# Dealing out the gather steps of the v stage by the weight megabytes that TensorE still has ahead of it

## The chip, the cores and the metric

The kernel runs on one core of one Trainium2 chip. The metric is the device time of one execution in microseconds. Three runs of the kernel before took 2020.26, 2021.27 and 2027.03 us; their median, 2021.27 us, is the time to compare with.

## The reference

The program is a trunk of two layers over 256 tokens of width 1024. A layer has a mixer (convolution and pooling in layer 0, sparse attention beside a gated recurrence in layer 1), a cross attention over 256 memory rows, and the part that matters here, a layer of 16,384 experts of which each token chooses 128 (16 for each of 8 heads):

```python
def peer_ffn(h, wq, sub_keys, u, v):
    ...
        top, pos = lax.top_k(cand, PEER_TOPK)
        eid = jnp.take_along_axis(cand_id, pos, axis=-1).reshape(PEER_BLOCK, PEER_HEADS * PEER_TOPK)
        g = jax.nn.softmax(top, axis=-1).reshape(PEER_BLOCK, PEER_HEADS * PEER_TOPK).astype(xb.dtype)
        act = jax.nn.gelu(jnp.einsum('td,ted->te', xb, u[eid]))
        return jnp.einsum('te,ted->td', g * act, v[eid])
```

So a chosen expert e adds g · gelu(x·u[e]) · v[e] to the token. u and v are 64 MB each in a layer.

## The kernel before

The expert layer is the function `peer`, called once in each layer. It treats the 256 tokens in two ways.

176 tokens (`TD`) are done densely: all of u and all of v go through TensorE (PE). u and v are cut into 64 *pairs* (`NPAIR`) of two blocks of 128 experts. One pair is a `raw` tile of 128 partitions by 2048 fp32 values, 1 MB (2 to the power of 20 bytes), which `load` (line 774) fetches by SP's queue into one of five buffers in turn. `u_range` (line 819) computes the u half: it loads a pair of u, does its two blocks of matmuls at line 827 with a `yield` after each, and lets ScalarE (ACT) apply gelu at line 833. `v_pair` (line 1118) does the v half: VectorE (DVE) multiplies the activations by the gate weights into a `wt` tile (line 1130, three buffers), and PE adds the products into the four PSUM banks `O` (line 1134). The first 20 pairs (`NFIRST`) keep their weighted activations in `af` and need no `wt`. The gate weights of the others lie in HBM (`gd`) and come back four pairs at a time into `gr` (line 1116, two buffers), by SP's queue too, one group ahead.

The other 80 tokens (`NG`, in groups of 64 and 16) are done by *gather steps*. The generator `gathered` (line 793) has 160 of them in a layer. One step is an indirect DMA on GpSimd's queue (POOL, line 790) that fetches one expert row for each of 128 partitions (128 rows of 4 KB), and one DVE instruction that uses it: in the first 80 steps a dot product with the token (line 797, `dots`), in the last 80 a weighted sum into `acc` (line 809; the first step of a group at line 807). The row tiles share eight buffers, so a gather is issued when the DVE instruction of the step eight before it is done. When a group's sums are complete, PE adds them into the result by the `fold` matmuls at line 1175, and the result is added to `h` at line 1184.

The order: the u pairs 0 to 19 run beside the choosing of the experts; the rest of their 40 halves, 19, carry one gather step each; then `spread` builds the gate weights with the u pairs 20 to 39 beside it and a step after every second turn, which makes another 19. The code has thus taken 38 steps when the *v stage* begins. The v stage goes through the 64 v pairs in an order written out in `order` (first six of the af pairs, then the pairs 20 to 63 with one more af pair after every third) and runs the last 24 u pairs, 40 to 63, beside the first 24 v pairs from 20 on: 88 MB through PE in all. After each v pair it takes one gather step, after every fourth pair two: 80 in the stage. What is left is taken after the loop, 42 steps.

DVE's order inside these loops is the order of the program (`manual_schedule`); the other engines' queues are ordered by the framework's scheduler, and each queue runs in order. In the loop a DVE step of iteration n therefore stands behind `wt` of iteration n and ahead of `wt` of iteration n+1, and `wt` waits until PE has freed the buffer of three `wt` before it.

Of the kernel before, what the change touches and what calls it, by code (L numbers as in the profile page):

```python
# [28 lines left out]
NPAIR = 64  # L29
TG = 16  # L30
NFIRST = 20
NACT = 20

GROUPS = ((0, 64), (64, 16))
NG = sum(n for _, n in GROUPS)
TD = T - NG
NHEAD = 6
GQ = 4
Q1 = 2.2
Q2 = 1.7  # L40
# [28 lines left out]
def trunk(ctx: ExitStack, tc: tile.TileContext, a: dict, out: bass.AP, dbg=None):  # L69
# [37 lines left out]
    def bank():  # L107
        return ps.tile([P, 512], F32, name="b", tag="ps", bufs=2)
# [625 lines left out]
    def peer(l, sq, fill=None):  # L734
        with ExitStack() as es:
# [35 lines left out]
            turn = [0, 0]  # L771


            def load(src):

                n = turn[0] % 5
                turn[0] += 1
                if n < 3:
                    raw = st.tile([P, 2048], F32, name="raw", tag="raw", bufs=3)
                else:  # L780
                    raw = cp.tile([P, 2048], F32, name="raw", tag=f"xT{n - 3}", bufs=1)
                nc.sync.dma_start(raw, src)
                return raw

            def rows(src, g, i):

                q = ("whi", "wlo")[turn[1] % 2]
                turn[1] += 1
                t = st.tile([P, D], F32, name="row", tag=q, bufs=4)
                nc.gpsimd.indirect_dma_start(t, None, src, bass.IndirectOffsetOnAxis(ap=g["gi"][:, i:i + 1], axis=0))  # L790
                return t

            def gathered():
                for g in gs_:
                    for i in range(g["n"]):
                        t = rows(u_rows, g, i)
                        nc.vector.tensor_tensor_reduce(t, t, g["xg"], 1.0, 0.0, OP.mult, OP.add, g["dots"][:, i:i + 1])  # L797
                        if i == g["n"] - 1:
                            nc.scalar.activation(g["dots"], g["dots"], AF.Gelu_apprx_tanh)
                            nc.vector.tensor_mul(g["gw"], g["gw"], g["dots"])  # L800
                        yield
                for gn, g in enumerate(gs_):
                    acc = g["acc"] = pp.tile([P, D], F32, name=f"acc{gn}", tag=f"ga{gn}")
                    for i in range(g["n"]):
                        t = rows(v_rows, g, i)
                        if i == 0:
                            nc.vector.tensor_scalar(acc, t, g["gw"][:, 0:1], None, op0=OP.mult)
                        else:
                            nc.vector.scalar_tensor_tensor(acc, t, g["gw"][:, i:i + 1], acc, op0=OP.mult, op1=OP.add)  # L809
                        yield  # L810
# [8 lines left out]
            def u_range(i, j):  # L819

                for i in range(i, j):
                    raw = load(a["peer_u"][l, i])
                    b = bank()
                    for c in range(2):
                        for k in range(KB):
                            o = c * 1024 + k * P
                            nc.tensor.matmul(b[:, c * TD:(c + 1) * TD], raw[:, o:o + P], xd[:, k], start=k == 0, stop=k == KB - 1)  # L827
                        if c == 1:
                            if i < NFIRST:
                                dst = af[:, 2 * i:2 * i + 2].rearrange("p c t -> p (c t)")  # L830
                            else:
                                dst = act[i] = pools["ex"].tile([P, 2 * TD], F32, name="act", bufs=NACT)
                            nc.scalar.activation(dst, b[:, :2 * TD], AF.Gelu_apprx_tanh)  # L833
                            done.append(dst)
                        yield
# [197 lines left out]
            us = u_range(0, NFIRST)  # L1033
            interleave(choose(), us, Q1)
            bg = gathered()

            def steps():
# [64 lines left out]
            us = u_range(NFIRST, NFIRST + NACT)  # L1102
# [10 lines left out]
            def weights_of(g):  # L1113
                if g < (NPAIR - NFIRST) // GQ:
                    gr[g] = vp.tile([P, TD // TG, GQ * 2 * TG], F32, name="gr", bufs=2)
                    nc.sync.dma_start(gr[g], gd[:, :, g * GQ * 2 * TG:(g + 1) * GQ * 2 * TG].rearrange("g p f -> p g f"))

            def v_pair(i, first, last):
                if i < NFIRST:
                    raw = load(a["peer_v"][l, i])  # L1120
                    wt = af[:, 2 * i:2 * i + 2]
                else:
                    g, j = divmod(i - NFIRST, GQ)
                    if j == 0:
                        weights_of(g + 1)
                    gv = gr[g][:, :, j * 2 * TG:(j + 1) * 2 * TG].rearrange("p g (c t) -> p c g t", c=2)
                    raw = load(a["peer_v"][l, i])
                    at = act.pop(i)
                    wt = vp.tile([P, 2, TD], F32, name="wt", bufs=3)
                    nc.vector.tensor_mul(wt.rearrange("p c (g t) -> p c g t", t=TG),  # L1130
                                         at.rearrange("p (c g t) -> p c g t", c=2, t=TG), gv)
                parts = [(c, j) for c in range(2) for j in range(KB)]
                for c, j in sorted(parts, key=lambda z: z[1]) if last else parts:
                    nc.tensor.matmul(O[j // 2][:, (j % 2) * TD:(j % 2 + 1) * TD], raw[:, c * 1024 + j * P:c * 1024 + (j + 1) * P],  # L1134
                                     wt[:, c], start=first and c == 0 and j % 2 == 0, stop=last and c == 1,
                                     skip_group_check=True)
                if last:
                    ready_sqrt(wt[:, 0, 0:1])


            order, late = list(range(NHEAD)), list(range(NHEAD, NFIRST))
            for i in range(NFIRST, NPAIR):
# [2 lines left out]
                    order.append(late.pop(0))  # L1145
            order += late
            us = u_range(NFIRST + NACT, NPAIR)
            with tc.manual_schedule(engines={nc.vector.engine}):
                for n, i in enumerate(order):
                    v_pair(i, n == 0, n == NPAIR - 1)  # L1150
                    if n == 1:
                        weights_of(0)
                    for _ in range(2 if n % 4 == 3 else 1):
                        next(bg, None)
                    if i >= NFIRST:
                        next(us, None)
                        next(us, None)
            for _ in bg:
                pass

# [58 lines left out]
    with ExitStack() as es:  # L1219
# [7 lines left out]
        left = [(l, c) for l in range(2) for c in range(8)]  # L1227
# [27 lines left out]
        dump("h_xa0", h)  # L1255
        fill(6)
    sq = peer(0, sq)
    dump("h_pe0", h)
    sq = odd_mixer(sq)
    dump("h_mix1", h)  # L1260
    with phase("kv1") as kp:
# [4 lines left out]
        sq = xattn(1, k1, v1, sq)  # L1266
    dump("h_xa1", h)
    sq = peer(1, sq)


# [101 lines left out]
```

## Time and profile before

| what | value |
|---|---|
| median of three runs | 2021.27 us |
| profiled execution, its own time | 2011.56 us |
| its span, first to last instruction | 2009.3 us |
| mean granted clock of PE | 0.97 |
| busy: PE, DVE, ACT, POOL | 1885.8, 1090.7, 447.2, 409.5 us |
| moved by DMA | 572.76 MB, mean 285 GB/s |
| v stage of layer 0, layer 1 (first to last matmul of line 1134) | 537 to 957, 1534 to 1954 us of the span |

Times inside the profile are microseconds from the first instruction. One engine's row gives busy time; a PE that is busy is not PE at its peak, because matmuls overlap. In a timeline row the first number is the start, the second the length of the merged pieces, and the bracket tells how long the engine had been idle before them and what it had waited for. Windows give, for a stretch, each engine's busy time, PE's granted clock as a share of full speed, the mean busy share of the 16 DMA engines (packets can overlap, so it can pass 1) and the bytes moved per second.

### The profile page before, as it was taken

Reading aid. Unit: us, or ns where it says so; the run is one execution under the profiler, and the core shown is the slowest. Engines: PE = TensorE matmul, PEld = TensorE weight load, DVE = VectorE, ACT = ScalarE, POOL = GpSimd, SP = SyncE. Lnnn points to the kernel's source line nnn. Section 1 sums busy time; section 2 is a strip of 40 time slices with the busy share of each in tenths; the row PEclk is TensorE's granted clock in tenths of the full one; section 3 lists DMA queues with packets and bytes.
Section 4 is the critical chain, followed back from the end, with each engine's and each line's share of the span. In section 5 each row is a group of like instructions: output and inputs, shape, how many; then the busy total and the mean of one; then the engine's idle time right before and its main releaser. Section 6 shows DMA issues by size and latency. Waiting matters only on the chain.

```text
span 2009.3 us, 33483 instructions
## 1 busy us (share of the span) xinstructions
PE 1885.8 (94%) x13818; PEld 1856.6 (92%) x13818; DVE 1090.7 (54%) x2494; ACT 447.2 (22%) x807; POOL 409.5 (20%) x360
## 2 busy tenths in 40 slices
PE   8999999999899999999299999999989999999992
PEld 7999999999899999999199899999989999999981
DVE  5765588676512222345878766985765121213467
ACT  6455442122100000000074455421221000000000
POOL 0000001432211111234600100014322121212344
PEclk9999999999999999999599999999999999999996
DMA  6554756999998899899863254579999889988997
GB/s 242 182 186 137 243 176 220 372 383 342 352 335 306 319 309 335 313 379 345 342 218 116 106 214 141 176 267 364 372 336 364 318 311 318 326 313 329 381 343 272
DMA packets 138631, 572.76 MB, mean 285 GB/s; under 512 B 12400, under 2 KB 47984, under 8 KB 94960
## 3 DMA queue, kind: packets, MB, share of 16 engines
q1 hardware_dynamic: 81008, 370.06, 50.6%
q0 software_dynamic: 46080, 167.79, 22.7%
q10 hardware_dynamic: 11392, 32.77, 4.3%
q8 instruction: 109, 1.79, 0.3%
q14 instruction: 42, 0.34, 0.0%
HBM read 549.48 MB, written 21.10 MB: 284 GB/s over the span
## 4 chain that ended last, share of the span: by engine, by line
PE 52%; issue 27%; DVE 8%; POOL 6%; DMA 5%; ACT 1%; DVEq 0%; POOLq 0%; ACTq 0%
PE O L1134 14%; PE b L148 13%; PE b L827 11%; PE b L163 7%; POOL row L790 6%; DMA row<-in_peer_ur_dram,gi 2%; DVE acc L809 2%; DMA row<-in_peer_v_dram,gi 1%; DMA kd<-kvs 1%; DVE row L797 1%; DMA vd<-kvs 1%; PE fb L869 1%; PE fb L312 1%; PE fa L281 1%; PE fb L552 1%
## 5 line engine op out<-in xcount | busy, mean ns | idle before, releaser
L827 PE MATMUL b<-xd,raw 128*128 128x176 f32 x4096 | 634.7, 315 | 0.7 <-ACT af L833 0.7
L827 PEld LDWEIGHTS b<-xd,raw 128*128 128x128 f32 x4096 | 618.1, 191 | 1.2 <-ACT af L833 1.2
L1134 PE MATMUL O<-wt,raw 128*128 128x176 f32 x2816 | 430.2, 313 | 0.0
L1134 PEld LDWEIGHTS O<-wt,raw 128*128 128x128 f32 x2816 | 422.6, 190 | 0.0
L1130 DVE TENSOR_TENSOR wt<-act,gr 128x352 f32<-128x352 f32 x88 | 46.2, 525 | 589.9 <-PE O L1134 563.7
L790 POOL DMA_INDIRECT row<-in_peer_ur_dram,gi x160 | 196.8, 1230 | 802.2 <-DVE dots L797 482.1
L790 POOL DMA_INDIRECT row<-in_peer_v_dram,gi x160 | 192.7, 1205 | 352.6 <-DVE acc L809 224.6
L148 PE MATMUL b<-xT,whi 128*128 128x256 f32 x1376 | 250.2, 283 | 2.8 <-DVE xT L129 2.4
L126 DVE TENSOR_TENSOR wlo<-raw,whi 128x1024 fp32r<-128x1024 f32 x158 | 191.2, 1220 | 101.6 <-ACT whi L125 100.9
L148 PEld LDWEIGHTS b<-xT,whi 128*128 128x128 f32 x1376 | 211.7, 189 | 5.2 <-DVE xT L129 3.8
L125 ACT ACTIVATE whi<-raw 128x1024 fp32r<-128x1024 f32 x158 | 166.1, 1060 | 217.7 <-PE b L148 117.9
L797 DVE CUSTOM_DVE_ANT_0 row<-row,xg 128x1024 f32<-128x1024 f32 x160 | 191.9, 1214 | 41.1 <-DMA row<-in_peer_ur_dram,gi 41.1
L809 DVE SCALAR_TENSOR_TENSOR acc<-row,gw,acc 128x1024 f32<-128x1024 f32 x156 | 200.1, 1283 | 7.7 <-DMA row<-in_peer_v_dram,gi 4.1
L1134 PE MATMUL O<-af,raw 128*128 128x176 f32 x1280 | 195.8, 313 | 0.0
L148 PE MATMUL b<-xT,wlo 128*128 128x256 f32 x688 | 192.5, 280 | 0.3 <-DVE wlo L126 0.3
L1134 PEld LDWEIGHTS O<-af,raw 128*128 128x128 f32 x1280 | 192.2, 190 | 0.0
L833 ACT ACTIVATE act<-b 128x352 f32<-128x352 f32 x88 | 40.9, 464 | 652.7 <-PE b L827 652.7
L148 PEld LDWEIGHTS b<-xT,wlo 128*128 128x128 f32 x688 | 129.7, 189 | 0.8 <-DVE wlo L126 0.5
L163 PE MATMUL b<-whi,y 128*128 128x256 f32 x512 | 89.4, 279 | 0.0
L1175 PE MATMUL b<-acc,fold 128*128 128x512 f32 x16 | 14.2, 1016 | 75.4 <-DVE acc L809 75.4
L1175 PEld LDWEIGHTS b<-acc,fold 128*128 128x128 f32 x16 | 4.2, 308 | 81.1 <-issue 44.3
L163 PEld LDWEIGHTS b<-whi,y 128*128 128x128 f32 x512 | 77.4, 188 | 0.4
(333 smaller groups left out, 1766.5 us busy)
## 6 DMA issues: line engine op xcount, KB each, us to landing
raw<-in_peer_u_dram SPq DMA_DIRECT2D x128, 1024.0 KB, 7.9
raw<-in_peer_v_dram SPq DMA_DIRECT2D x128, 1024.0 KB, 7.5
raw<-in_xattn_wkv_dram SPq DMA_DIRECT2D x16, 1024.0 KB, 5.0
raw<-in_peer_wq_dram SPq DMA_DIRECT2D x16, 1024.0 KB, 5.0
gd<-gs ACTq DMA_DIRECT2D x22, 704.0 KB, 8.7
gr<-gd SPq DMA_DIRECT2D x22, 704.0 KB, 9.7
raw<-in_odd_w_in_dram SPq DMA_DIRECT2D x15, 1024.0 KB, 4.9
raw<-in_even_w_in_dram SPq DMA_DIRECT2D x8, 1024.0 KB, 4.8
```

The costliest lines, as they stand in the source:

```text
L125: nc.scalar.activation(hi, src, AF.Copy)
L126: nc.vector.tensor_sub(lo, src, hi.bitcast(F32))
L148: nc.tensor.matmul(dst, w[j][p][:, k * P:(k + 1) * P], x[q][:, k, :], start=n == 0, stop=n == 3 * KB - 1)
L163: nc.tensor.matmul(dst, x[q][:, k, tb * P:(tb + 1) * P], wk[p][:, o:o + 256], start=n == 0, stop=n == 3 * KB - 1)
L281: nc.tensor.matmul(lg[:, tb * T:(tb + 1) * T], qT[p][:, 2 * hd + j, tb * P:(tb + 1) * P], kT[q][:, 2 * hd + j], start=n == 0, stop=n == 5)
L790: nc.gpsimd.indirect_dma_start(t, None, src, bass.IndirectOffsetOnAxis(ap=g["gi"][:, i:i + 1], axis=0))
L797: nc.vector.tensor_tensor_reduce(t, t, g["xg"], 1.0, 0.0, OP.mult, OP.add, g["dots"][:, i:i + 1])
L809: nc.vector.scalar_tensor_tensor(acc, t, g["gw"][:, i:i + 1], acc, op0=OP.mult, op1=OP.add)
L827: nc.tensor.matmul(b[:, c * TD:(c + 1) * TD], raw[:, o:o + P], xd[:, k], start=k == 0, stop=k == KB - 1)
L833: nc.scalar.activation(dst, b[:, :2 * TD], AF.Gelu_apprx_tanh)
L1130: nc.vector.tensor_mul(wt.rearrange("p c (g t) -> p c g t", t=TG), at.rearrange("p (c g t) -> p c g t", c=2, t=TG), gv)
L1134: nc.tensor.matmul(O[j // 2][:, (j % 2) * TD:(j % 2 + 1) * TD], raw[:, c * 1024 + j * P:c * 1024 + (j + 1) * P], wt[:, c], start=first and ...
```

## The change

It replaces the fixed deal of one step per iteration (two on every fourth) by a count in units of 1 MB of weights. A v pair is one unit, a u pair that runs beside it another, so the stage has 88 units. `left` is 85 of them, all but the last three (`NTAIL`), and `todo` is the number of gather steps not yet taken when the stage begins (`turn[1]` counts those that are), 160 − 38 = 122. Each unit adds `per` = 122/85 = 1.435 to `due`, and as many steps are taken as `due` holds whole ones. The u pair of an iteration now comes ahead of its gather steps in the program; before, it came behind them.

```diff
+NTAIL = 3
...
+            left, todo = 2 * NPAIR - NFIRST - NACT - NTAIL, 2 * NG - turn[1]
+            due, per = 0.0, todo / left
             with tc.manual_schedule(engines={nc.vector.engine}):
                 for n, i in enumerate(order):
                     v_pair(i, n == 0, n == NPAIR - 1)
                     if n == 1:
                         weights_of(0)
-                    for _ in range(2 if n % 4 == 3 else 1):
+                    due += per
+                    if i >= NFIRST and next(us, "no") != "no":
+                        next(us, None)
+                        due += per
+                    while due >= 1:
+                        due -= 1
                         next(bg, None)
-                    if i >= NFIRST:
-                        next(us, None)
-                        next(us, None)
             for _ in bg:
                 pass
```

Nothing else is changed; the steps, the loads and the matmuls are the same in number and kind.

## Rows read from the trace of the kernel before

**Rows 1.** The page: the span in 40 slices of 50 us, the busy share in tenths (9 is 90% or more) of PE and of the DMA engines.

```profile
PE   8999999999899999999299999999989999999992
...
DMA  6554756999998899899863254579999889988997
```

**Rows 2.** The timeline, in order of time, at the end of the expert layer of layer 0: start us, length us, engine, line, operation, written tile and read tiles, count, and in brackets the idle time before and its releaser.

```profile
938.64 17.13 DVE L809 SCALAR_TENSOR_TENSOR acc<-row,gw,acc 128x1024 f32<-128x1024 f32 x13
...
947.47 9.71 PE L1134 MATMUL O<-wt,raw 128*128 128x176 f32 x64
...
952.44 5.10 SPq L134 DMA_DIRECT2D raw<-in_odd_w_in_dram  x2
...
958.63 0.52 DVE L1164 COPY ob<-O 128x352 f32<-128x352 f32 x1
...
979.24 3.75 PE L1175 MATMUL b<-acc,fold 128*128 128x512 f32 x4 [22.06 <-DVE acc L809]
...
999.87 2.08 PE L1175 MATMUL b<-acc,fold 128*128 128x512 f32 x2 [16.88 <-DVE acc L809]
...
1003.69 0.69 DVE L1184 TENSOR_TENSOR h<-b,h 128x512 f32<-128x512 f32 x1 [2.74 <-PE b L1180]
```

**Rows 3.** The same view at the end of layer 1.

```profile
1944.46 9.71 PE L1134 MATMUL O<-wt,raw 128*128 128x176 f32 x64
...
1973.82 3.71 PE L1175 MATMUL b<-acc,fold 128*128 128x512 f32 x4 [19.65 <-DVE acc L809]
...
1994.39 2.08 PE L1175 MATMUL b<-acc,fold 128*128 128x512 f32 x2 [16.86 <-DVE acc L809]
```

**Rows 4.** The instructions on the row tiles from 537 to 1000 us (minimum, median and maximum ns of one, first and last start), and the group of the `acc` instructions from 340 to 1000 us (busy us, mean ns).

```profile
L797 DVE CUSTOM_DVE_ANT_0 row<-row,xg x35: 1216/1218/1221, 546.2 to 758.3; 128x1024 f32<-128x1024 f32 x35
L790 POOL DMA_INDIRECT row<-in_peer_ur_dram,gi x27: 934/939/1681, 547.7 to 715.7; - x27
...
L809 DVE SCALAR_TENSOR_TENSOR acc<-row,gw,acc 128x1024 f32<-128x1024 f32 x78 | 100.1, 1283 | 5.1 <-DMA row<-in_peer_v_dram,gi 3.3
```

**Rows 5.** The chain that ended last, in layer 0's v stage: start us, length us, what. 32 matmul instructions are one pair.

```profile
570.54 4.77 PE b L827 x32
...
828.30 105.03 PE O L1134 x704
```

**Rows 6.** Windows: the stretch and its length, then busy us (and instructions) of PE, PE's weight loads, DVE, ACT and POOL, PE's granted clock, the DMA share, GB/s. The first five lie in v stages; the next three in the stages of u, with PE busy throughout; the last begins as PE's v stage has ended.

```profile
537.00:957.00 420.00, 420.00 (x2817) 419.91 (x2816) 124.98 (x167) 14.56 (x31) 102.32 (x85) 1.00 0.92 331
570.00:637.00 67.00, 67.00 (x451) 67.00 (x450) 14.59 (x26) 2.79 (x6) 12.34 (x10) 1.00 0.90 316
637.00:704.00 67.00, 67.00 (x451) 67.00 (x450) 14.81 (x27) 3.04 (x7) 11.60 (x10) 1.00 0.86 309
840.00:930.00 90.00, 90.00 (x605) 90.00 (x604) 36.94 (x38) 0.00 (x0) 32.55 (x25) 1.00 0.99 375
1840.00:1930.00 90.00, 90.00 (x606) 90.00 (x605) 36.58 (x38) 0.00 (x0) 31.74 (x24) 1.00 0.99 378
380.00:410.00 30.00, 30.00 (x203) 30.00 (x202) 12.99 (x30) 2.79 (x6) 11.86 (x9) 1.00 1.01 409
430.00:450.00 20.00, 20.00 (x171) 19.85 (x168) 14.90 (x37) 5.23 (x12) 3.75 (x4) 1.00 1.02 420
1380.00:1410.00 30.00, 30.00 (x203) 30.00 (x203) 14.15 (x34) 3.12 (x7) 11.49 (x9) 1.00 1.01 402
957.00:980.00 23.00, 0.94 (x3) 0.50 (x2) 19.38 (x17) 0.00 (x0) 17.33 (x15) 0.57 1.02 411
```

**Rows 7.** The page's DMA part: the queue of the gathers (packets, MB, share of 16 engines), and the `gr` loads (count, KB each, median us to landing).

```profile
q0 software_dynamic: 46080, 167.79, 22.7%
...
gr<-gd SPq DMA_DIRECT2D x22, 704.0 KB, 9.7
```

**Rows 8.** Time from issue to landing. First the weight loads (`raw`) issued from 840 to 930 us and from 380 to 410 us, then the gathered rows issued from 840 to 930, from 380 to 410 and from 410 to 500 us.

```profile
DMA to landing us min/median/max: 6.8/8.3/10.7
DMA to landing us min/median/max: 6.8/8.2/8.5
DMA to landing us min/median/max: 6.0/9.1/11.2
DMA to landing us min/median/max: 7.2/12.9/14.0
DMA to landing us min/median/max: 6.9/9.9/18.8
```

**Rows 9.** The window and the timeline around a place where PE waited, in layer 0's `spread`.

```profile
500.00:510.00 10.00, 4.69 (x41) 4.36 (x39) 4.80 (x9) 1.48 (x4) 2.45 (x4) 0.81 0.90 349
...
505.20 1.22 DVE L797 CUSTOM_DVE_ANT_0 row<-row,xg 128x1024 f32<-128x1024 f32 x1 [5.75 <-DMA row<-in_peer_ur_dram,gi]
...
507.93 0.27 PE L1083 MATMUL fa<-A,B 128*128 128x128 f16 x1 [4.97 <-DVE A L1072]
```

**Rows 10.** The timeline of the v stage of layer 0: the `wt` of pair 61, and SP's queue around a load of `gr`.

```profile
923.87 0.53 DVE L1130 TENSOR_TENSOR wt<-act,gr 128x352 f32<-128x352 f32 x1 [1.74 <-PE O L1134]
...
838.43 0.38 SPq L1116 DMA_DIRECT2D gr<-gd  x1
842.65 19.42 SPq L782 DMA_DIRECT2D raw<-in_peer_v_dram  x5
```

**Rows 11.** All fold matmuls of both layers: minimum, median and maximum ns of one, first and last start.

```profile
L1175 PE MATMUL b<-acc,fold x16: 592/1061/1222, 979.2 to 1998.3; 128*128 128x512 f32 x16
```

## The prediction

> **What bounds the kernel now.** I read the page's slices first. PE is busy nine tenths or more nearly everywhere, but one slice of each layer falls to two tenths: the one in which the expert layer ends, while the DMA engines stay full [rows 1]. The timeline of these two places shows why. In layer 0 the last v matmul ends at 947.47 + 9.71 = 957.18 us, and the fold of the second token group starts at 999.87, after waiting for `acc` [rows 2]. In layer 1 the same two points are 1944.46 + 9.71 = 1954.17 and 1994.39 [rows 3]. PE thus waits 42.69 and 40.22 us for gather steps that the loop left over, 82.91 us in all, but for short folds of the first group in between.
>
> The stage itself is set by PE: it is busy 420.00 of 420 us from 537 to 957 [rows 6], at 4.77 us a pair [rows 5], and 88 x 4.77 = 420. Beside it DVE works 125 us and POOL 102 [rows 6], and the DMA engines move 309 to 316 GB/s while u pairs run along and 375 to 378 afterwards [rows 6]. So the steps of the tail could be hidden under PE if the DMA engines can carry them; that is the question of this forecast.
>
> **The change part by part.** *What goes.* 42 steps leave the tail. Of the 82.91 us not all goes. The folds of the first group, 3.75 us and 3.71 us, now lie inside the wait [rows 2, 3]; afterwards they stand behind the last v matmul. Bounds: nothing, if the scheduler puts them ahead of PE's end, and 3.75 us with the slow matmuls that follow idle time. The fastest fold took 592 ns [rows 11], and four make 2.4 us; I take that, since PE will not have idled, and so 42.69 - 2.4 + 40.22 - 2.4 = 78.1 us. What is late next: the copies of the `O` banks, the last at 958.63 + 0.52 us, 2 us after PE's end [rows 2], beside the folds; and the next layer's first weights, issued at 952.44 [rows 2], which at 8.3 us [rows 8] land at about 961, while the sum into `h`, 3.8 us after the last fold begins, comes at about 962 and the norm that makes the next matmuls' other operand follows it. I charge neither.
>
> *What is added inside the stage.* DVE gets 42 x 1.28 us [rows 4] = 54 us more, 179 of 420. PE never waits for DVE's sum, only for its order, so this costs nothing as long as rows land in time. The steps now end with the unit count 85, in the iteration of pair 61, so behind its `wt`, which stood at 923.87 [rows 10]: 33 us ahead of PE's end, against a few us for the last steps' own work. Before the first `wt` the loop now has 8 steps where it had 7 (6 units x 1.435), one more in a place where DVE waits for `gr` anyway; DVE had done 45 dots by then, since only 35 follow [rows 4], which is 38 + 7. Cost from 0 to the 5.75 us that DVE once waited for a row there [rows 9]; I take 0.
>
> *The rows' load on DMA.* A gather moves 167.79 MB / 320 = 0.524 MB [rows 7]. While u pairs run along, 7 units (33.4 us) hold 4 iterations: 5 steps before, 7 x 1.435 = 10.05 after. The 5.05 extra steps are 2.65 MB, or 79 GB/s, on a mean of 312: 392 GB/s. Afterwards an iteration is one unit of 4.77 us with 1.435 steps instead of 1.25: 0.097 MB more, 20 GB/s, on 376: 396 GB/s. Can the DMA engines do that with PE fed? In the stages of u they carried the same mixture, one step per 2.4 us of PE, at 409, 420 and 402 GB/s while PE was busy 30 of 30, 20 of 20 and 30 of 30 us [rows 6]. With gathers almost alone they reached 411 [rows 6]. So the demand lies 2 to 6% under what was seen; `gr` loads, absent there, narrow that.
>
> *Slack when they are full.* Eight row buffers and a step every 4.77 / 1.435 = 3.32 us give a gather 26.6 us to land; under full load it took 12.9 us at the median and 18.8 at most [rows 8]. Weight loads have five buffers, four pairs or 19 us ahead, and landed within 8.5 us at 409 GB/s [rows 8]. A late row delays the next `wt`, which runs three buffers ahead of PE. Cost of PE stalls: below, 0, and not less, as PE is already busy throughout the stage. Above, let 376 GB/s, which the stage itself held for 90 us at a DMA share of 0.99 [rows 6], be a ceiling: 234 us (570 to 804, seven periods) at 392/376 and 84 us (840 to 924) at 396/376 stretch by 9.6 + 4.4 = 14 us a layer. I take 1.5 us a layer, 3 in all, near the lower end, because the nearest rows of the same mixture are those at 402 to 420.
>
> The Trainium skill's page "DMA: Bandwidth & Descriptors", section "Specifications", speaks against the change: it gives the HBM limit of one core as about 358 GB/s, below the demand of 392 to 396. An estimate by that page: 392/358 on 234 us and 396/358 on 84 us is 31 us a layer, 62 in all. The trace does not agree where it can be asked: 402 to 420 GB/s over 20 to 30 us [rows 6]; that a lower limit shows only over longer times is not excluded by these rows.
>
> *Queues.* POOL's gathers keep their order; it needs 0.94 us for one at the median [rows 4] and has 3.3. On SP nothing is added, but `gr` waits there for a `wt` of DVE, with `raw` loads behind it: at 838.43 and 842.65 [rows 10] it cost no time, as the loads came with PE's pace.
>
> *The sum.* The profiled execution took 2011.56 us (span 2009.3): 2011.56 - 78.1 + 3 = 1936.5. The median of the runs stands 9.71 us above it, and I take the same for after: **1946 us**.
>
> **The rivals.** *DMA becomes the bound, mildly.* The stage sticks at its own 376 GB/s, PE waits 14 us a layer: 1943 + 28 = 1971 us. For it: a share of 0.99 already [rows 6]. Against: share does not measure what is left, as the same engines carry 411 GB/s at 1.02 [rows 6]. *A ceiling of 358*, lasting over hundreds of us: 1943 + 62 = 2005 us, little ahead of before. Against it are all rows above 358. *The change doesn't do what it says*: DVE's order or the count `turn[1]` leaves some steps behind the loop. 44 steps took from 938.64 to 999.87 [rows 2], 1.39 us each; with 21 left over the sums end 29 us after DVE's last `wt` (938), so 10 us after PE's end instead of 43: about 1966 us. The rows speak against it, as 38 + 7 + 35 dots add up.
>
> *Slower than before.* DVE takes its work in order, so a row that lands late holds up `wt` and, through the buffer of `gr`, SP's queue with the weight loads behind; PE then starves. One such wait of 5.75 us for a row cost PE 10 - 4.69 = 5.31 us in `spread` [rows 9], at a place with less lead. If each of the 11 `gr` groups of each layer met it, that would be 22 x 5.31 = 117 us: 1943 + 117 = 2060. It decides from 15 such stalls on (78.1 / 5.31). Against it: in the v stage `wt` leads by three pairs, and rows have 26.6 us where the worst took 18.8.
>
> **How the numbers follow.** Forecast 0.72, mild DMA bound 0.16, ceiling of 358 0.03, steps left over 0.04, starving PE 0.05. The first four are faster by more than 0.3% (6 us, about what can be told from no change): 0.95. Of the last, 0.04 is slower and 0.01 lies between. The lower end is the whole 82.91 us gone and most of the 9.71 too, 1930; the upper covers 1971 with some 15 us for uneven filling, 1985. Outside lie the ceiling, the starving and some ends of the rest.
>
> **What would show it.** Right: PE's gap between the last v matmul and the folds under 4 us in both layers; 1.435 steps a unit, the last `acc` some 30 us before PE's end; 385 to 400 GB/s between 570 and 800 us; v stages of 420 to 425 us; row landings up to 20 us. Wrong: PE idle before matmuls of line 1134 or 827 with `wt` or `raw` as releaser, v stages of 435 us or more, windows stuck at 360 to 376 GB/s, or `acc` instructions still behind PE's end.

## The result and the profile after

The changed kernel took 1935.86 us (median of four runs, 1931.80 to 1937.96), the kernel before 2020.76 in the same comparison (four runs, 2017.44 to 2027.03): a ratio of 0.9574, 95% interval 0.9545 to 0.9602. The forecast was 1946 us, range 1930 to 1985. The profiled execution took 1936.71 us, its span is 1934.5.

The page's slices after, with the rate below them; the two slices of PE's wait [rows 1] are gone, and the DMA engines are nine tenths busy or more right through the v stages:

```profile
PE   8999999999899999999999999999998999999998
...
DMA  6544655799999999999463353568999999999992
GB/s 244 181 175 153 223 186 203 297 385 375 346 392 404 396 403 386 399 352 390 163 215 120 110 218 131 174 220 324 389 349 348 383 410 401 395 391 376 363 374 98
```

The timeline at the end of layer 0, to be set beside [rows 2]:

```profile
927.86 2.60 DVE L811 SCALAR_TENSOR_TENSOR acc<-row,gw,acc 128x1024 f32<-128x1024 f32 x2
...
951.02 9.71 PE L1136 MATMUL O<-wt,raw 128*128 128x176 f32 x64
...
960.56 1.88 PE L1182 MATMUL b<-acc,fold 128*128 128x512 f32 x4
...
964.25 0.69 DVE L1191 TENSOR_TENSOR h<-b,h 128x512 f32<-128x512 f32 x1
```

The last `acc` is done at 930.5, 30 us ahead of PE's end, and the folds follow the last v matmul at once. The windows of the v stages, to be set beside [rows 6] (the third, fourth and fifth are the stretches with u pairs, the sixth the late part):

```profile
541.00:961.00 420.00, 420.00 (x2816) 419.76 (x2815) 162.01 (x196) 14.35 (x32) 135.30 (x111) 1.00 0.95 365
1503.00:1923.00 420.00, 420.00 (x2809) 418.72 (x2808) 162.90 (x197) 14.07 (x30) 134.26 (x107) 1.00 0.94 362
574.00:641.00 67.00, 67.00 (x451) 67.00 (x450) 26.32 (x48) 3.03 (x7) 24.68 (x20) 1.00 1.03 407
641.00:708.00 67.00, 67.00 (x451) 67.00 (x450) 27.68 (x32) 2.99 (x7) 24.49 (x20) 1.00 1.02 400
708.00:775.00 67.00, 67.00 (x451) 67.00 (x450) 28.49 (x27) 2.78 (x6) 24.92 (x20) 1.00 1.01 387
844.00:934.00 90.00, 90.00 (x605) 90.00 (x604) 39.52 (x41) 0.00 (x0) 24.85 (x20) 1.00 0.94 362
```

PE is busy 420.00 of 420 us in both layers: the steps cost the stage nothing. Three marks divide the span: the first u matmul of a layer, its first v matmul, and the first sum into `h` behind the folds. From the first to the second I call it u stage below, from the second to the third v part.

| profile | u stage, layer 0, 1 | v part, layer 0, 1 | span |
|---|---|---|---|
| before | 229.7, 230.7 | 466.7, 464.1 | 2009.3 |
| after | 232.5, 236.4 | 423.8, 422.9 | 1934.5 |

The v parts give 42.9 + 41.2 = 84.1 us; the u stages, which the change touches by one step alone, took 8.5 us of it back. What slowed the u stages stays open; the run `again` tells whether it comes back.

### The profile page after: what moved, and what is told of

Read it like the earlier page. It is cut to its first block, busy times and chain, and to the rows that moved or that the text cites. A ratio compares the mean times of both kernels' runs of the same rounds, so it can differ in the third digit from the quotient of the medians.

```text
span 1934.5 us, 33505 instructions
## 1 busy us (share of the span) xinstructions
PE 1883.2 (97%) x13818; PEld 1858.7 (96%) x13818; DVE 1091.6 (56%) x2494; ACT 446.8 (23%) x807; POOL 421.0 (22%) x360
## 4 chain that ended last, share of the span: by engine, by line
PE 77%; DVE 8%; issue 8%; DMA 4%; POOL 2%; ACT 1%; another core or an unknown queue 0%; DVEq 0%; ACTq 0%; POOLq 0%
PE O L1136 32%; PE b L829 17%; PE b L149 15%; PE b L164 6%; DMA row<-in_peer_ur_dram,gi 2%; POOL row L791 2%; DMA vd<-kvs 1%; PE fb L871 1%; PE fb L313 1%; PE fa L282 1%; PE fb L553 1%; DVE big L971 1%; PE fb L222 0%; DVE wlo L127 0%; DVE cs L976 0%
## 5 line engine op out<-in xcount | busy, mean ns | idle before, releaser
L791 POOL DMA_INDIRECT row<-in_peer_v_dram,gi x160 | 200.6, 1254 | 366.0 <-DVE acc L811 288.1
L164 PE MATMUL b<-wlo,y 128*128 128x256 f32 x256 | 70.6, 278 | 0.0
```

Source lines behind the costliest of these rows:

```text
L164: nc.tensor.matmul(dst, x[q][:, k, tb * P:(tb + 1) * P], wk[p][:, o:o + 256], start=n == 0, stop=n == 3 * KB - 1)
```

## The experiments

All ran beside the kernel before. `again`, `no_tail`, `by_pair` and `early` shared one chip and its runs of the kernel before; `ntail0`, `late_start`, `pace75` and `u_after` followed together on the same chip, `edge` and `both` on another. The three theories of the expectations are A (the gain is the tail's wait, the stage carries the steps for nothing), B (the growth of the u stages belongs to the change) and C (the steps cost something in the stage).

| run | median us | ratio to before, interval |
|---|---|---|
| `again` | 1925.30 | 0.9579 (0.9557 to 0.9600) |
| `no_tail` | 1927.38 | 0.9591 (0.9572 to 0.9609) |
| `by_pair` | 1941.38 | 0.9653 (0.9626 to 0.9681) |
| `early` | 2001.18 | 0.9952 (0.9935 to 0.9969) |
| `ntail0` | 1928.36 | 0.9593 (0.9575 to 0.9611) |
| `late_start` | 1912.42 | 0.9513 (0.9498 to 0.9529) |
| `pace75` | 1925.35 | 0.9585 (0.9568 to 0.9603) |
| `u_after` | 1926.62 | 0.9577 (0.9558 to 0.9597) |
| `edge` | 1935.11 | 0.9622 (0.9606 to 0.9638) |
| `both` | 1910.25 | 0.9502 (0.9486 to 0.9518) |

**The change once more.** No edit.

> The changed kernel once more, beside the kernel before on the same chip. It tells how much of the 84.9 us of the first comparison is scatter, and whether the 2.9 and 5.8 us by which the stages of u grew in the first profile come back. Theory A (the gain is the tail's wait, the stage carries the steps for nothing): ratio 0.955 to 0.962, v stages of 420 us, a gap of under 4 us between the last v matmul and the folds. Theory B (the growth of the stages of u belongs to the change): the v stage of layer 0 starts at 540 us or later again; if it is scatter it starts anywhere between 536 and 541.

The kernel before stood at 2010.81 us here, the gain at 85.5. The u stages were 229.8 and 230.7 us, those of before, and the v parts 423.7 and 422.8. A holds, B falls: the growth belongs to the first comparison, where both kernels took some 10 us more than here, and not to the change.

**No tail at all.**

```diff
-            for _ in bg:
-                pass
...
-                        for gn, g in enumerate(gs_):
+                        for gn, g in enumerate(gs_[:1]):
```

> The kernel before without the 42 steps behind the loop: the last 42 rows of v and the folds of the second token group are left out, so the sums are incomplete. It is what the change could gain if the steps moved into the stage cost nothing there. Theory A: within 0.4% of the changed kernel, 1925 to 1940 us (two folds a layer less, 2.4 us in both layers). Theory C (the steps cost something in the stage by their load on DMA): 10 us or more below the changed kernel, under 1925 us.

Leaving the 42 steps out gains no more than moving them: 1927.38 against 1925.30, 0.1% apart with overlapping intervals. A holds and C falls; the change has taken the whole of what the tail cost.

**Dealt by iterations.**

```diff
-            left, todo = 2 * NPAIR - NFIRST - NACT - NTAIL, 2 * NG - turn[1]
+            left, todo = NPAIR - NTAIL, 2 * NG - turn[1]
...
                         next(us, None)
-                        due += per
```

> The changed kernel with the same 122 steps dealt out by iterations instead of megabytes: two in each of the first 61 iterations. While u pairs run along the DMA engines then carry less (about 345 GB/s), afterwards 220 + 220 + some 25 = 465 GB/s would be wanted. Theory A with a ceiling of about 410 GB/s: DVE falls behind in the last part, the windows there stand at 400 to 415, and the v stage grows by 3 to 12 us a layer: 1940 to 1960 us. Rival (no ceiling that matters, because rows have lead enough): as the changed kernel within 3 us. Rival of a starving PE: stops before matmuls of 10 us and more in many pairs, over 1980 us.

16 us above `again`, inside the range of A: the v parts are 431.1 and 433.6 us instead of 423.7 and 422.8. The window of the late part, and a piece of the chain of waits (start, length, what) inside it:

```profile
844.00:934.00 90.00, 85.58 (x556) 85.31 (x555) 49.13 (x48) 0.00 (x0) 37.13 (x28) 0.96 1.02 402
```

```profile
865.17 23.44 DMA raw<-in_peer_v_dram
```

PE loses 4.42 us there, waiting for a weight load that took 23.4 us to land. So it is the count by megabytes, and not only the emptied tail, that keeps PE fed: without it 16 of 85 us are lost.

**Finished early.**

```diff
-NTAIL = 3
+NTAIL = 28
```

> The changed kernel with the steps finished 28 units before the end instead of 3, so 122/60 = 2.03 steps a unit, 220 + 223 + 16 = 459 GB/s wanted while u pairs run along. Theory A with a ceiling of about 410: the excess of 49 GB/s over some 260 us is 12.8 MB, 31 us of DMA time a layer; the eight rows in flight hide a part, PE stops for 5 to 25 us a layer: 1946 to 1986 us, windows at 400 to 415 and DVE waiting for rows. Rival of a starving PE: over 2000 us. Rival that no ceiling matters: as the changed kernel within 3 us.

2001 us: nearly the whole gain is lost, more than A allowed and in the band of the starving PE. Windows while u pairs run along; what PE waited for from 540 to 1000 us (us in total, times, longest); then the queues from 580 to 760 us (q0 the gathers, q1 SP's loads: packets, MB, share) and the median landing of u loads:

```profile
641.00:708.00 67.00, 59.84 (x378) 59.37 (x377) 35.13 (x31) 2.23 (x5) 31.60 (x28) 0.95 1.03 408
708.00:775.00 67.00, 62.41 (x407) 62.15 (x406) 33.02 (x29) 2.78 (x6) 28.11 (x23) 0.97 1.03 411
```

```profile
PE O L1136 <- DMA raw<-in_peer_v_dram: 13.2, 2, 8.6
PE b L829 <- DMA raw<-in_peer_u_dram: 11.5, 3, 4.3
```

```profile
q0 software_dynamic: 10341, 37.66, 53.1%
q1 hardware_dynamic: 10177, 35.59, 49.5%
...
raw<-in_peer_u_dram SPq DMA_DIRECT2D x14, 1024.0 KB, 19.7
```

The ceiling is here to be read: 408 to 411 GB/s at a share of 1.03. The weight loads then land after 19.7 us, when their lead is 19, and PE stops for 3.0 to 8.6 us five times a layer (2.8 to 9.6 us in layer 1). SP's queue and PE around the first stop:

```profile
571.80 0.33 SPq L783 DMA_DIRECT2D raw<-in_peer_u_dram  x1
582.16 0.38 SPq L1118 DMA_DIRECT2D gr<-gd  x1
582.65 5.39 SPq L783 DMA_DIRECT2D raw<-in_peer_v_dram  x2
...
604.22 8.02 PE L1136 MATMUL O<-af,raw 128*128 128x176 f32 x32 [8.59 <-DMA raw<-in_peer_v_dram]
612.08 4.94 PE L1136 MATMUL O<-wt,raw 128*128 128x176 f32 x32
```

Here SP's queue stood for 10.0 us with `gr` waiting for a `wt` of DVE, and DVE had been waiting for rows, some 11 us in all between 562 and 580; the load behind `gr` was issued late and then took 21.5 us. Layer 1 has the same once, with 9.8 us. The other four stops of a layer come without such a hold, but each waits, like the first, for the load that stands right behind a `gr` in SP's queue; so do all stops of `by_pair` and `edge` in their v stages. What the 0.72 MB of a `gr` ahead of a load are worth was not run. Behind the stop 32 matmuls take 8.02 us in place of 4.94, at a granted clock of 0.62 on average from 604.0 to 612.3 us, so mostly at the lower of its two levels (1.2 and 2.4 GHz).

The v part of layer 0 is 460.4 us, 36.7 more than in `again`; 60 units of 4.77 us stretched by 459/409 give 35. My expectation of 5 to 25 us was wrong because it let the rows' lead hide 26 us: a lead delays a stop and does not pay for an excess that lasts.

**The last three pairs not kept free.**

```diff
-NTAIL = 3
+NTAIL = 0
```

> The changed kernel without the clause on the last three pairs: 122/88 = 1.386 steps a unit, right up to the last pair. Theory A: DVE takes its last steps behind the wt of pair 63, some 19 us ahead of PE's end, so the folds wait for nothing: as the changed kernel within 0.3% (6 us), gap under 4 us. Rival (the last three pairs have to be kept free, or the rows are late for the folds): 5 to 15 us slower than the changed kernel, with PE waiting for acc before the folds.

1928.36, with its companions `u_after` and `pace75` at 1926.62 and 1925.35: no difference that can be told. DVE's last `acc` ends at 939.6, PE's last v matmul at 955.5: DVE runs that far ahead anyway, and the clause does not bring the gain.

**The old place of the u pair.**

```diff
-                    due += per
-                    if i >= NFIRST and next(us, "no") != "no":
-                        next(us, None)
-                        due += per
+                    due += per * (2 if NFIRST <= i < NPAIR - NACT else 1)
                     while due >= 1:
                         due -= 1
                         next(bg, None)
+                    if i >= NFIRST:
+                        next(us, None)
+                        next(us, None)
```

> The changed kernel's deal with the old place of the u pair, behind the gather steps of its iteration. Theory A: nothing on DVE depends on it, as a u pair gives DVE no work: as the changed kernel within 0.3%. Rival (part of the gain comes from u pairs issued ahead of the steps): 6 us or more slower.

1926.62, as A says: the order of the two in the program is worth nothing.

**Fewer steps ahead of `spread`.**

```diff
-            interleave(steps(), iter(()), 1.0, bg, 1.0)
+            interleave(steps(), iter(()), 1.0, bg, 0.75)
```

> The changed kernel with three steps for four half pairs of u instead of four in the short stretch between the choosing and the building of the gate weights: 220 + 165 = 385 GB/s wanted there instead of 440, and 127 steps left, 1.49 a unit, 400 GB/s, in the v stage. Theory A with a ceiling of 409: DVE no longer falls behind in that stretch, the stop of PE for a late row behind it (5 us a layer) goes or shrinks, and the v stage still holds its 420 us: 3 to 10 us faster than the changed kernel of the same chip. Rival (the stop has another cause): no change, or slower by the larger load on the v stage.

No change: 1925.35, u stages of 230.2 and 228.6 us. The stop of PE in `spread` does not come from this stretch, and A fell on this point.

**No step for the first six pairs.**

```diff
-            left, todo = 2 * NPAIR - NFIRST - NACT - NTAIL, 2 * NG - turn[1]
+            left, todo = 2 * NPAIR - NFIRST - NACT - NTAIL - NHEAD, 2 * NG - turn[1]
...
-                    due += per
+                    due += per if n >= NHEAD else 0
```

> The changed kernel with no step in the first six iterations (the af pairs, whose 8 steps DVE takes ahead of time, during the building of the gate weights): 122/79 = 1.544 steps a unit afterwards, 220 + 170 + 16 = 406 GB/s wanted against the 409 that the early kernel showed as the ceiling. If the stop of PE in the stage of u (some 5 us a layer) comes from these steps, the kernel gains up to 5 us a layer: 1915 us. Theory A says that it comes from the steps before them (one for every 2.4 us of PE, 440 GB/s wanted), so the stop stays, and the v stage is at the edge of the ceiling: 1923 to 1935 us.

1912.42 us, a larger gain than the first alternative gave with 1915, and the reverse of what I had put on A. The u stages fell from 229.8 and 230.7 (`again`) to 221.9 in both layers; the v parts stayed at 423.6 and 422.9. Between the medians the gain is 12.9 us. In `again` DVE's place in `spread` looks like this, with PE behind it and the window below:

```profile
506.16 1.22 DVE L799 CUSTOM_DVE_ANT_0 row<-row,xg 128x1024 f32<-128x1024 f32 x1 [4.48 <-DMA row<-in_peer_ur_dram,gi]
...
508.89 0.27 PE L1085 MATMUL fa<-A,B 128*128 128x128 f16 x1 [4.85 <-DVE A L1074]
```

```profile
500.00:540.00 40.00, 34.82 (x274) 34.23 (x273) 25.97 (x59) 8.31 (x18) 13.01 (x11) 0.91 0.94 364
```

The window of `late_start`, and two of its v stage:

```profile
500.00:540.00 40.00, 40.00 (x327) 39.69 (x327) 17.17 (x41) 8.31 (x18) 4.17 (x4) 1.00 0.92 336
574.00:641.00 67.00, 67.00 (x452) 67.00 (x451) 28.74 (x52) 3.03 (x7) 27.60 (x22) 1.00 1.03 408
641.00:708.00 67.00, 67.00 (x451) 67.00 (x451) 30.01 (x37) 2.90 (x7) 27.39 (x22) 1.00 1.03 409
```

The steps of the first six iterations have no `wt` ahead of them, so DVE takes them during `spread`, between the products that PE waits for. There a row that is late stops PE. Without them PE is busy 40.00 of 40 us, and the v stage carries the steps at 408 to 409 GB/s with PE still full: right at the ceiling, and not over it.

**Over the edge, and a little under it.** Both start from `late_start`:

```diff
-NTAIL = 3
+NTAIL = 11
```

> The kernel of late_start with the steps finished 11 units before the end: 122/71 = 1.718 steps a unit, 220 + 189 + 16 = 425 GB/s wanted while u pairs run along and some 437 afterwards. If the stage stretches in the ratio of what is wanted to a ceiling of 409, once the loads in flight are used up: 267 us at 425/409 and some 72 us at 437/409 are 10 + 5 = 15 us a layer at most, 5 us less where the buffers hide a part: 20 to 30 us above late_start, 1932 to 1942 us, with PE waiting for weight loads. Rival (row buffers give lead enough for a short excess): within 5 us of late_start, 1907 to 1918 us. Rival (equal shares of two full queues, so that the weights drop at once to half of 409, 205 GB/s, against 220): 7% of 340 us, 24 us a layer, 1955 us and more.

```diff
-NTAIL = 3
+NTAIL = 0
```

> No step in the first six iterations and none kept back at the end: 122/82 = 1.488 steps a unit, 400 GB/s wanted. It adds room under the ceiling to late_start. Theory: as late_start within 0.3%, 1907 to 1918 us, v stages of 420 us. Rival (late_start at 406 GB/s already loses time to the ceiling): 3 us or more faster than late_start.

`edge` took 1935.11 us; its v parts are 437.6 and 435.3 us, 14.0 and 12.4 above those of `late_start`, against the 10 to 15 that the ratio to 409 gave. Both rivals fall. Two of its windows:

```profile
574.00:641.00 67.00, 62.46 (x400) 62.22 (x399) 29.58 (x54) 2.57 (x6) 30.50 (x24) 0.95 1.03 407
708.00:775.00 67.00, 64.02 (x427) 63.78 (x426) 33.63 (x31) 2.78 (x6) 28.91 (x25) 0.99 1.03 406
```

19 GB/s more than in `late_start` are wanted, and the rate stays at 406 and 407: PE pays. `both` took 1910.25 us, as `late_start` within its interval, with v parts of 423.7 and 422.9. It and `late_start` beat both kernels of the comparison; the rest of the room (400 instead of 406 GB/s wanted) is not worth time that can be told here.

## Why the prediction was right or wrong

**What bounds the kernel: right.** PE's wait of 82.91 us for left-over steps was the cost; `no_tail` shows that nothing else was to be had from them.

**What goes, 78.1 us: too small, 84.1.** The step that failed is the 2.4 us a layer that I gave back for the first group's folds. From the end of the last v matmul to the sum into `h` it was 46.5 us in layer 0 [rows 2] and is 964.25 - 960.73 = 3.5. The folds do stand there now, but the four ahead of the first sum, two of each group, take 1.88 us together, less than the 2.08 that the second group's two took before at the lowered clock [rows 2]: a PE that has not idled pays for the first group's itself.

**PE stalls in the stage, 3 us: none.** The windows show 420.00 of 420 in both layers. That the nearest rows were those at 402 to 420 GB/s was right, and the ceiling of 376 that I used as the upper end is not one: the stage ran at 387 to 407, and at up to 411 in `early`. (The stretch that I worked out from 376 is 10.0 + 4.5 = 14.5 us a layer, not 9.6 + 4.4 = 14, which changes nothing.) The rival with 376 falls, and so does the one with 358 GB/s (the limit in "Specifications" of "DMA: Bandwidth & Descriptors" in the Trainium skill): the stage held 408 to 409 GB/s over 134 us in `late_start`. The load while u pairs run along came as worked out, 387 to 407 against 392. The late part did not: 362 against 396, as the rows are fetched eight steps ahead of DVE and the last gather was issued at 905.5, inside the window.

**The slack when the queues are full: wrong in the reason.** I read 8.5 us for a weight load at 409 GB/s [rows 8] as what full queues cost. Those stretches lasted 30 us. Where they stay full (`early`), the load takes 19.7 us. How the engines divide their rate between two full queues these runs do not show. The same page of the Trainium skill says in "Queues, rings and completion order" that an engine takes its queues in turn, packet by packet; no run here shows it, since packets and bytes followed what the program dealt: 10341 and 10177 packets, 37.66 and 35.59 MB for gathers and loads in `early`, which deals them about equally, but 11157 and 13266 packets, 40.62 and 50.62 MB in `edge` (574 to 800 us), which deals 0.90 MB of rows to 1.13 of loads. The starving rival was therefore a real one. Its mechanism, a late row that holds `wt`, `gr` and SP's queue in turn, shows before the longest stop of each layer of `early`; the other stops come from weight loads that land late without it. Both appear where the wanted rate passes 409 GB/s for long. The change wants 392 and lies 4% below.

**The steps ahead of the first `wt`, 0: right as a difference, and the largest thing missed.** The eighth step cost nothing that `again` shows. But I read the 5.3 us that PE lost there [rows 9] as a property of the place; `late_start` shows that such steps cause it, at 8 to 9 us a layer of the profiled executions.

**The offset of 9.71 us: sound, and the profiled sum met by luck.** The profiled execution before, 2011.56 us, is none of the runs of the first comparison (2017.44 to 2027.03); it lies among those of the later ones (2003.69 to 2015.58). The one after, 1936.71, is a run of the first comparison itself, 0.85 us above its median. So the two profiles do not stand on the same level, and that the profiled sum of 1936.5 met 1936.71 is chance: 84.1 - 78.1 = 6.0 us too little gained and 3 us of stalls that did not come cancel against 8.5 us that the u stages took longer there. Median against median the forecast gained 2021.27 - 1946 = 75.3 us and the change 2020.76 - 1935.86 = 84.9 (85.5 in `again`). The forecast's 10 us too many are thus, but for 1 us, the 6.0 and the 3, and not the offset.

**The clause that the steps are left over, and the order of the u pair:** neither mattered (`acc` ends 30 us early; `u_after`).

## What to carry to other kernels

Background transfers that share the DMA engines with the bound engine's own loads should be dealt by the bytes that engine still has to take, so that the sum stays just under the ceiling all along: 406 GB/s cost nothing, 425 cost 12 to 14 us a layer, 459 cost 37. Buffers in flight carry a short burst; an excess that lasts is paid nearly in full by the ratio of what is wanted to the ceiling. That ratio gives 35 us a layer for `early` (36.7 measured) and at most 15 for `edge` (14.0 and 12.4); for the shorter excess of `by_pair`, 23 pairs of 4.77 us at about 465/409, it gives an estimated 15, of which 7.4 and 10.8 were paid. And where a loop's first iterations have nothing to wait for, look where an engine that works in order takes their background work: here it stood in an earlier stage, in front of products that TensorE needed.

## What the runs showed that was not expected

A DMA share of 0.99 at 375 to 378 GB/s [rows 6] is not full: the same engines carried 400 to 411 at 1.01 to 1.03. And a stop of PE costs more than its length: in `early` PE waited 24.7 us for weight loads in layer 0, but its v part grew by 36.7. The 32 matmuls behind each of the five stops took 6.7 to 8.0 us instead of 4.9, 11.3 us in all, at a lowered clock.
